# Where the softmax of a differential attention, its filler's vector work and the modulation rows stand in the issue order

## Chip, cores, metric

One core of one Trainium2 chip (trn2). The metric is the device time of one execution in microseconds (us), the median over runs of the same kernel. Engines: PE (TensorE, matmuls), DVE (VectorE), ACT (ScalarE), POOL (GpSimd), SP (which here issues most of the loads). Each engine works through its own queue in order and waits on semaphores for the others.

## What is computed

One layer of a decoder trunk on x of 512 x 1024 (fp32): a modulated RMSNorm, one input projection that feeds two token mixers (sliding-window attention A, differential attention B), a gated merge, and a gated MLP with a short causal convolution. Cut to what matters here:

```python
mod = cs @ w_ada[l] + b_ada[l]                      # 6 x 1024 modulation values
shift1, scale1, gate1, shift2, scale2, gate2 = ...
h = _rmsnorm(x, norm1_g[l]) * (1.0 + scale1) + shift1
proj = h @ w_in[l]
qa, ka, va, qd, kd, vd, ga, gd = jnp.split(proj, points, axis=-1)
...
# _diff_attention, for each block of 128 queries, 4 heads, 2 maps (m) of 64 dimensions
scores = jnp.einsum('bqhmd,bshmd->bhmqs', qblk, k).astype(jnp.float32) * scale
scores = scores - slopes[:, None, None, None] * delta.astype(jnp.float32)
scores = jnp.where(delta >= 0, scores, NEG_INF)
p = jax.nn.softmax(scores, axis=-1)
a = p[:, :, 0] - lam * p[:, :, 1]
return jnp.einsum('bhqs,bshe->bqhe', a.astype(v.dtype), v)
```

The change computes the same.

## The kernel before

**Products.** Every fp32 product is made of three matmuls (`mm3`, L118 to L120): each operand is split into a high part `hi`, an ACT cast to the matmul's type, and a low part `lo = src - hi`, a DVE subtraction (`split`, L114 and L115). PE multiplies weight hi by activation hi (L118), weight hi by activation lo (L119) and weight lo by activation hi (L120); only the third reads the low part of the weight. Weight chunks of 512 KB come by `load_cols` (L464): a raw buffer (tag `raw`, four buffers, shared with the modulation rows), a load on SP, then the split into `whi` and `wlo` (three buffers each).

**The stage.** PE's order in the stage is written by hand (`tc.manual_schedule`); the queues of the other engines are ordered by a scheduler from program order, priorities and dependencies. `tc.high_priority` raises what is traced in it. Small attention matmuls alternate with big ones: `fill(n)` gives out n ticks. A tick runs the next step of the current unit (one k-step of a projection chunk: the query, key and value chunks of the next head `pq`, `pk`, `pw`, or a gate chunk `pga` and a branch chunk `pA`) and keeps two more units' weights loaded ahead. A tick also counts down the callbacks of `after(n, fn)`, and every eighth tick (`ADA_EVERY`) advances the generator `ada_rows` by one step.

**Modulation rows.** The MLP's modulation values are not needed in the attention stage, and `ada_rows` makes them piece by piece: eight half rows of 512 columns (`arow` 00, 01, 10 ... in the text: row, half). A step loads two 128 x 512 slices of `w_ada` (`ra`, L741, on SP), and DVE multiplies each by its value of `cs` and adds it to `arow` (L746, L748). After four steps the half row is split into `arh` and `arl` (L115), and one tick later (`ADA_LAG`) `ada_spread` sums over the partitions by two matmuls on PE (`pr`, L757 for `arh`, L758 for `arl`), ACT copies the row out (L760) and POOL writes it to `mod_rows` (L761). `arow` has one buffer: a new half row begins when the one before has been written.

**Differential attention.** The loop at the end of the listing goes over 16 blocks s = 4h + n (head h, block n of 128 queries). `diff_scores` makes the two maps' scores on PE (L125) and reduces each to its maximum on DVE while adding the mask and the distance penalty (L664; the tile is `sd`, the maximum `dmx`). `diff_softmax` scales the maximum (L676), takes two exponentials on ACT with their sums (L678), and combines the maps on DVE (L681 to L684); L684 leaves the block's probabilities. `diff_transpose` turns them on PE (`td`, L693) and splits them into `aTh` (ACT, L424) and `aTl` (DVE, L425). `diff_values` multiplies by the values (`od`). In a turn of the loop, before: two filler ticks; the scores of the block or blocks ahead; four filler ticks; the transposes of s; the softmax of the block or blocks ahead; in a head's first block also the values of the head before, and two ticks. Ahead of the loop: the scores and softmaxes of blocks 0 and 1, then three ticks.

Of the kernel before, what the change touches and what calls it, by code (L numbers as in the profile page):

```python
# [11 lines left out]
ALU = mybir.AluOpType  # L12
# [15 lines left out]
HP = 100000  # L28
# [8 lines left out]
DIFF_FILL = (3, 2, 4, 2)  # L37
# [15 lines left out]
def kernel(  # L53
# [22 lines left out]
    nc = tc.nc  # L76
# [15 lines left out]
    def fbank(name):  # L92
        return bank("f", 2, [P, S], name)

    def sbank(name, shape=(P, S)):
        return bank("s", 3, list(shape), name)
# [7 lines left out]
    def raw_tile(shape, name):  # L104
        return wp.tile(shape, F32, tag="raw", bufs=4, name=name)

    def split_pair(raw, shape, name):
        hi = wp.tile(shape, F32R, tag="whi", bufs=WB, name=name + "_h")
        lo = wp.tile(shape, F32R, tag="wlo", bufs=WB, name=name + "_l")
        split(hi, lo, raw)  # L110
        return hi, lo
# [10 lines left out]
    def mm3_rows(groups):  # L122
        for a, b, start, stop in ((0, 0, True, False), (0, 1, False, False), (1, 0, False, True)):
            for o, lhs, rhs in groups:
                nc.tensor.matmul(o, lhs[a], rhs[b], start=start, stop=stop)  # L125
# [251 lines left out]
    for gi, g in enumerate(groups):  # L377
        nxt = groups[gi + 1] if gi + 1 < len(groups) else ()
# [83 lines left out]
    def load_cols(src, col, name):  # L462
        r = raw_tile([P, KT, P], name)
        nc.sync.dma_start(r, src[:, col : col + P].rearrange("(a p) n -> p a n", p=P))  # L464
        return split_pair(r, [P, KT, P], name)
# [11 lines left out]
    def prefetch():  # L477
        while units and len(loaded) < 2:
            load, run = units.pop(0)
            loaded.append((load(), run))  # L480

    def fill(n):
        for _ in range(n):
            if not current:
                prefetch()
                if loaded:
                    wts, run = loaded.pop(0)
                    current.append(run(wts))
                    prefetch()
            if current:  # L490
                try:
                    next(current[0])
                except StopIteration:
                    current.clear()
            for e in list(later):
                e[0] -= 1
                if e[0] <= 0:
                    later.remove(e)
                    e[1]()
            tick[0] += 1  # L500
            if tick[0] >= ADA_START and tick[0] % ADA_EVERY == 0:
                next(ada, None)

    def after(n, fn):
        later.append([n, fn])
# [1 line left out]
    def steps(o, wts, rhs, nk, k0=0, cl=slice(0, P)):  # L507
        wh, wl = wts
        for k in range(nk):
            mm3(o, wh[:, k, cl], wl[:, k, cl], rhs[0][k0 + k], rhs[1][k0 + k], k == 0, k == nk - 1)  # L510
            if k < nk - 1:
                yield
# [126 lines left out]
    def diff_scores(*ss):  # L639
        ops = []  # L640
        for s in ss:
            h, n = divmod(s, NT)
            t = heads[h]
            w = (n + 1) * P
            if n == 0:
                firsts[h] = [sbank(f"sd{h}_{m}", (P, 2, 256)) for m in range(2)]
            sps = [firsts[h][m][:, n, :w] if n < 2 else sbank(f"sd{h}_{n}_{m}")[:, :w] for m in range(2)]
            mm3_rows([
                (
                    sps[m],  # L650
                    [t[64 * m : 64 * m + 64, b, n * P : (n + 1) * P] for b in range(2)],
                    [t[64 * m : 64 * m + 64, 2 + b, :w] for b in range(2)],
                )
                for m in range(2)
            ])
            ops.append((s, sps, w))
        for s, sps, w in ops:
            h, n = divmod(s, NT)
            mx = ap.tile([P, 2], F32, tag="dmx", bufs=3, name=f"dmx{h}_{n}")
            pm = []  # L660
            for m in range(2):
                st = ap.tile([P, w], F32, tag="st", bufs=ST, name=f"sd{h}_{n}_{m}")
                with tc.high_priority(offset=HP):
                    nc.vector.tensor_tensor_reduce(  # L664
                        st, sps[m], ddf[:, 512 - w : 512], 1.0, -3e38, ALU.add, ALU.max, mx[:, m : m + 1]
                    )
                pm.append(st)
            scored[s] = mx, pm

    def diff_softmax(s):  # L670
        with tc.high_priority(offset=HP):
            h, n = divmod(s, NT)
            slope = 2.0 ** (-2 * (h + 1))
            mx, pm = scored[s]
            lsum = ap.tile([P, 2], F32, tag="dls", bufs=3, name=f"dls{h}_{n}")
            nc.vector.tensor_scalar_mul(mx, mx, -slope)  # L676
            for m in range(2):
                nc.scalar.activation(  # L678
                    pm[m], pm[m], AF.Exp, bias=mx[:, m : m + 1], scale=slope, accum_out=lsum[:, m : m + 1]
                )  # L680
            nc.vector.reciprocal(lsum, lsum)  # L681
            nc.vector.tensor_mul(lsum[:, 1:2], lsum[:, 1:2], nlam)
            nc.vector.tensor_scalar_mul(pm[1], pm[1], lsum[:, 1:2])
            nc.vector.scalar_tensor_tensor(pm[0], pm[0], lsum[:, 0:1], pm[1], ALU.mult, ALU.add)  # L684
            probs[s] = pm[0]

    def diff_transpose(s):
        h, n = divmod(s, NT)
        if n == 0:
            aTs[h] = [ap.tile([P, 1664], F32R, tag=g, bufs=2, name=f"{g}{h}") for g in ("aTh", "aTl")]  # L690
        tp = tbank(f"td{h}_{n}")
        for k in range(n + 1):
            nc.tensor.transpose(tp[:, k * P : (k + 1) * P], probs[s][:, k * P : (k + 1) * P], ident)  # L693
        hi, lo = (a.rearrange("p (b q) -> p b q", q=P)[:, n : 4 * n + 1 : 3] for a in aTs[h])
        with tc.high_priority(offset=HP):
            evac(hi, lo, tp[:, : (n + 1) * P].rearrange("p (k q) -> p k q", q=P))
# [69 lines left out]
    def add_gate_a(j):  # L766
        def gate(wts):
            o = fbank(f"pga{j}")
            yield from steps(o, wts, hT, KT)
            nc.scalar.activation(ta[:, j], o, AF.Tanh, scale=0.5)  # L770

        def load():
            if j % 2 == 0:
                r = raw_tile([P, 4, 2 * P], f"wba{j}")
                for a in range(2):
                    nc.sync.dma_start(
                        r[64 * a : 64 * a + 64],
                        wba[256 * a : 256 * a + 256, j * P : (j + 2) * P].rearrange("(i p) n -> p i n", p=64),
                    )
                pair_w["a"] = split_pair(r, [P, 4, 2 * P], f"wba{j}")  # L780
            return pair_w["a"]

        def branch(wts):
            o = fbank(f"pA{j}")
            rhs = [[outa[b][:, k] for k in range(4)] for b in range(2)]
            yield from steps(o, wts, rhs, 4, cl=slice(j % 2 * P, j % 2 * P + P))
            nc.vector.scalar_tensor_tensor(ta[:, j], ta[:, j], 1.0, o, ALU.add, ALU.mult)

        units.append((lambda: load_cols(win, COL_GA + j * P, f"wga{j}"), gate))
        units.append((load, branch))  # L790

    pairs, firsts, scored, probs, aTs = {}, {}, {}, {}, {}
    ada = ada_rows()
    add_head(0)
    add_head(1)
    fill(SWA_FILL[0])
    swa_scores(0, 0)
    fill(SWA_FILL[1])
    swa_scores(0, 2)
    swa_softmax(0)  # L800
    fill(SWA_FILL[2])
    for i in range(SWA_PAIRS):
        more = i + 1 < SWA_PAIRS
# [18 lines left out]
    ta = big.tile([P, KT, S], F32, tag="qa", name="ta")  # L822
    for j in range(2):
        add_gate_a(j)
    diff_scores(0, 1)
    diff_softmax(0)
    diff_softmax(1)
    fill(DIFF_FILL[0])
    for s in range(4 * DIFF_HEADS):
        h, n = divmod(s, NT)  # L830
        if n == 0 and 0 < h < 3:
            add_head(h + 1)
        elif s == 12:
            add_gate_a(2)
            add_gate_a(3)
        fill(DIFF_FILL[1])
        nxt = {0: (), 1: (s + 1,), 2: (s + 1,), 3: (s + 1, s + 2)}[n] if s < 15 else ()
        if nxt:
            diff_scores(*nxt)
        fill(DIFF_FILL[2])  # L840
        diff_transpose(s)
        for z in nxt:
            diff_softmax(z)
        if n == 0 and h:
            diff_values(h - 1)
            fill(DIFF_FILL[3])
    for j in range(4, KT):
        add_gate_a(j)
    fill(1)
# [923 lines left out]
```

## Time and profile before

| | us |
|---|---|
| median of 3 runs | 718.32 (717.43 to 718.40) |
| profiled execution | 719.43 |
| its span | 717.4 |
| PE busy | 690.6 |
| DVE busy | 588.9 |
| ACT busy | 383.6 |
| mean granted clock | 0.995 |

The span is what the profiler saw of the program; the profiled execution's time has 2.0 us more around it. The stage that the change touches lies between about 128 and 240 us of the span. In the profile's rows, `td<-ident,sd` means that the operation writes tile `td` and reads `ident` and `sd`; `[1.00 <-DVE qa L428]` is idle time ahead of the row and what ended it. The busy time of a matmul overlaps with its neighbours, since they are pipelined; the distance from one start to the next tells the rate: 0.23 us for a product of 512 columns in this stage.

### The profile page before, as it was taken

The page shows a single profiled execution, that of the slowest core. Times are in us where ns is not written, and L with a number is a line of the kernel's source. Part 1 is how long each engine was busy: PE and PEld are TensorE (multiplying, and loading weights), DVE is VectorE, ACT ScalarE, POOL GpSimd, SP SyncE. Part 2 cuts the span into 40 slices and gives each one's busy share as a digit, 9 for nine tenths or more (in the row PEclk, how much of TensorE's full clock was granted, in tenths as well). Part 3 has the DMA queues.
Part 4 walks back from the last instruction along what each step waited for, and adds up shares of the span by engine and source line. Part 5 has one row for each costly group of instructions (what it writes and reads, how often), then busy time and mean ns, then how long its engine had stood idle before and what let it go on. Part 6 is the DMA issues. An engine that isn't in the chain of part 4 may idle for free. (4 is left out here: it accounts for less than half of the span.)

```text
span 717.4 us, 11279 instructions
## 1 busy us (share of the span) xinstructions
PE 690.6 (96%) x4187; PEld 603.1 (84%) x4187; DVE 588.9 (82%) x1125; ACT 383.6 (53%) x677; POOL 84.0 (12%) x101
## 2 busy tenths in 40 slices
PE   5998899999999999999999999999999999999995
PEld 5776788877887888888879999999999999888884
DVE  5998877887986674875379999888889899979996
ACT  4643656455554233432358665556555666655664
POOL 4000000000100110000012021111111101540300
PEclk9999999999999999999999999999999999999998
DMA  9986122534544565726817689878779738997903
GB/s 310 301 251 205 60 59 61 176 110 126 176 114 151 183 195 182 233 90 211 245 52 156 157 179 210 200 187 219 190 191 230 168 121 237 183 203 194 161 0 118
DMA packets 115863, 121.82 MB, mean 170 GB/s; under 512 B 4415, under 2 KB 93280, under 8 KB 115808
## 3 DMA queue, kind: packets, MB, share of 16 engines
q1 hardware_dynamic: 96894, 95.09, 41.7%
q0 software_dynamic: 18720, 25.73, 21.4%
q8 instruction: 33, 0.54, 0.3%
q10 hardware_dynamic: 194, 0.28, 0.1%
q14 instruction: 22, 0.18, 0.1%
HBM read 118.97 MB, written 2.11 MB: 169 GB/s over the span
## 5 line engine op out<-in xcount | busy, mean ns | idle before, releaser
L1112 PE MATMUL up<-t,m_whi 128*128 128x256 f32 x528 | 96.1, 283 | 0.0
L1112 PEld LDWEIGHTS up<-t,m_whi 128*128 128x128 f32 x528 | 82.3, 192 | 0.0
L1112 PE MATMUL up<-t,m_wlo 128*128 128x256 f32 x264 | 74.7, 283 | 0.1
L1112 PE MATMUL up<-bh,p_wlo 128*128 128x256 f32 x232 | 65.7, 284 | 0.7 <-DVE p_wlo L1055 0.7
L1112 PE MATMUL up<-bh,p_whi 128*128 128x256 f32 x232 | 65.6, 283 | 0.0
L1112 PE MATMUL up<-bl,p_whi 128*128 128x256 f32 x232 | 65.6, 283 | 0.0
L1112 PEld LDWEIGHTS up<-t,m_wlo 128*128 128x128 f32 x264 | 50.6, 192 | 0.3 <-DVE m_wlo L1055 0.3
L1112 PEld LDWEIGHTS up<-bh,p_wlo 128*128 128x128 f32 x232 | 44.4, 192 | 1.1 <-DVE p_wlo L1055 1.1
L1112 PEld LDWEIGHTS up<-bl,p_whi 128*128 128x128 f32 x232 | 44.5, 192 | 0.0
L1112 PEld LDWEIGHTS up<-bh,p_whi 128*128 128x128 f32 x232 | 44.5, 192 | 0.0
L748 DVE SCALAR_TENSOR_TENSOR arow<-ra,cs,arow 128x512 f32<-128x512 f32 x56 | 41.9, 748 | 3.0 <-DMA ra<-in_w_ada_dram 2.3
L1023 POOL DMA_DIRECT2D s<-in_w_up_dram x21 | 27.2, 1385 | 143.2 <-DMA s<-in_w_up_dram 61.0
L1055 DVE TENSOR_TENSOR m_wlo<-s,m_whi 128x1024 fp32r<-128x1024 f32 x31 | 37.8, 1220 | 2.0 <-ACT m_whi L1051 2.0
L1051 ACT CAST m_whi<-s 128x1024 fp32r<-128x1024 f32 x31 | 32.4, 1046 | 9.4 <-DVE s L1045 6.0
L1112 PE MATMUL up<-t,p_whi 128*128 128x256 f32 x176 | 32.2, 283 | 0.0
L174 POOL TENSOR_TENSOR r<-ms,mhalf 128x1 f32<-128x1 f32 (+1 forms) x16 | 13.1, 820 | 143.2 <-DVE ms L172 76.5
L678 ACT ACTIVATE sd<-sd,dmx 128x128 f32<-128x128 f32 (+3 forms) x32 | 17.8, 557 | 22.1 <-DVE dmx L676 15.3
L761 POOL DMA_DIRECT2D mod_rows<-arow x8 | 4.3, 540 | 205.2 <-ACT arow L760 205.1
L1112 PEld LDWEIGHTS up<-t,p_whi 128*128 128x128 f32 x176 | 27.4, 192 | 0.2 <-issue 0.2
L1119 ACT ACTIVATE gT<-a,cv 128x512 f32<-128x512 f32 x22 | 17.7, 813 | 17.7 <-DVE a L1154 17.3
L1051 ACT CAST p_whi<-wa 128x1024 fp32r<-128x1024 f32 x18 | 18.7, 1040 | 12.0 <-PE up L1112 9.0
L1112 PE MATMUL up<-t,p_wlo 128*128 128x256 f32 x88 | 24.9, 283 | 0.0
(485 smaller groups left out, 2119.3 us busy)
## 6 DMA issues: line engine op xcount, KB each, us to landing
ra<-in_w_ada_dram SPq DMA_DIRECT2D x32, 512.0 KB, 4.0
wa<-in_w_up_dram SPq DMA_DIRECT2D x22, 512.0 KB, 4.3
s<-in_w_up_dram SPq DMA_DIRECT2D x21, 512.0 KB, 4.9
s<-in_w_up_dram POOLq DMA_DIRECT2D x21, 512.0 KB, 7.3
adaw<-in_w_ada_dram SPq DMA_DIRECT2D x16, 512.0 KB, 5.3
w<-in_w_in_dram SPq DMA_DIRECT2D x12, 512.0 KB, 3.9
a<-in_w_up_dram SPq DMA_DIRECT2D x11, 512.0 KB, 4.9
b<-in_w_down_dram SPq DMA_DIRECT2D x10, 512.0 KB, 3.8
```

The lines of the kernel that those rows point to most:

```text
L174: nc.gpsimd.tensor_tensor(r0, ms, mhalf[:, :n], ALU.pow)
L678: nc.scalar.activation(pm[m], pm[m], AF.Exp, bias=mx[:, m : m + 1], scale=slope, accum_out=lsum[:, m : m + 1])
L748: nc.vector.scalar_tensor_tensor(ac, r[:, a], cc, ac, ALU.mult, ALU.add)
L761: nc.gpsimd.dma_start(mod_rows[idx : idx + 1, hf * S : (hf + 1) * S], row)
L1023: nc.gpsimd.dma_start(dst, upblock(*blk), accum_op=ALU.add)
L1051: nc.scalar.copy(W[J, name][0], R[J, SRC[name]])
L1055: nc.vector.tensor_sub(lo, R[J, SRC[name]], hi.bitcast(F32))
L1112: nc.tensor.matmul(o[u], w[:, k, cu], b[:, k], start=name in ("p1", "m5", "p2") and k == 0 and x == 0, stop=k == 3 and x == 2, skip_group_ ...
L1119: nc.scalar.activation(grow(j), av[J][:, u], AF.Identity, bias=cv[:, 66 + j : 67 + j], scale=cv[:, 44 + j : 45 + j])
```

## The change

Five edits, all in issue order:

1. `diff_softmax` of the blocks ahead is called right behind their `diff_scores`, no longer behind the filler and the transposes.
2. `ends[s]` keeps the last DVE instruction of a softmax (L684 of before), `ends[s, "exp"]` its last exponential on ACT.
3. What is issued within `tc.issue_after(x)` and goes to the engine of instruction x is put behind x in that engine's queue. The fillers behind the scores (and the first three ticks) are issued within `issue_after(ends[...])` of the first of the new softmaxes.
4. In a head's block 1, the softmax itself is put behind that of block 0, on DVE and on ACT.
5. During the loop (`hold`), a step of `ada_rows` that a tick would run is only counted; `ada_due` runs the counted steps ahead of the four filler ticks, within `issue_after`.

```diff
--- before.py
+++ after.py
@@ -499,7 +499,16 @@
                     e[1]()
             tick[0] += 1
             if tick[0] >= ADA_START and tick[0] % ADA_EVERY == 0:
-                next(ada, None)
+                due[0] += 1
+                if not hold[0]:
+                    ada_due()
+
+    due, hold = [0], [False]
+
+    def ada_due():
+        while due[0]:
+            due[0] -= 1
+            next(ada, None)
 
     def after(n, fn):
         later.append([n, fn])
@@ -668,20 +677,23 @@
             scored[s] = mx, pm
 
     def diff_softmax(s):
-        with tc.high_priority(offset=HP):
+        with tc.high_priority(offset=HP), ExitStack() as order:
             h, n = divmod(s, NT)
+            if n == 1:
+                for key in (s - 1, (s - 1, "exp")):
+                    order.enter_context(tc.issue_after(ends[key]))
             slope = 2.0 ** (-2 * (h + 1))
             mx, pm = scored[s]
             lsum = ap.tile([P, 2], F32, tag="dls", bufs=3, name=f"dls{h}_{n}")
             nc.vector.tensor_scalar_mul(mx, mx, -slope)
             for m in range(2):
-                nc.scalar.activation(
+                ends[s, "exp"] = nc.scalar.activation(
                     pm[m], pm[m], AF.Exp, bias=mx[:, m : m + 1], scale=slope, accum_out=lsum[:, m : m + 1]
-                )
+                ).ins
             nc.vector.reciprocal(lsum, lsum)
             nc.vector.tensor_mul(lsum[:, 1:2], lsum[:, 1:2], nlam)
             nc.vector.tensor_scalar_mul(pm[1], pm[1], lsum[:, 1:2])
-            nc.vector.scalar_tensor_tensor(pm[0], pm[0], lsum[:, 0:1], pm[1], ALU.mult, ALU.add)
+            ends[s] = nc.vector.scalar_tensor_tensor(pm[0], pm[0], lsum[:, 0:1], pm[1], ALU.mult, ALU.add).ins
             probs[s] = pm[0]
 
     def diff_transpose(s):
@@ -789,7 +801,7 @@
         units.append((lambda: load_cols(win, COL_GA + j * P, f"wga{j}"), gate))
         units.append((load, branch))
 
-    pairs, firsts, scored, probs, aTs = {}, {}, {}, {}, {}
+    pairs, firsts, scored, probs, aTs, ends = {}, {}, {}, {}, {}, {}
     ada = ada_rows()
     add_head(0)
     add_head(1)
@@ -822,10 +834,12 @@
     ta = big.tile([P, KT, S], F32, tag="qa", name="ta")
     for j in range(2):
         add_gate_a(j)
+    hold[0] = True
     diff_scores(0, 1)
     diff_softmax(0)
     diff_softmax(1)
-    fill(DIFF_FILL[0])
+    with tc.issue_after(ends[0]):
+        fill(DIFF_FILL[0])
     for s in range(4 * DIFF_HEADS):
         h, n = divmod(s, NT)
         if n == 0 and 0 < h < 3:
@@ -837,13 +851,16 @@
         nxt = {0: (), 1: (s + 1,), 2: (s + 1,), 3: (s + 1, s + 2)}[n] if s < 15 else ()
         if nxt:
             diff_scores(*nxt)
-        fill(DIFF_FILL[2])
+            for z in nxt:
+                diff_softmax(z)
+        with tc.issue_after(ends[nxt[0]]) if nxt else ExitStack():
+            ada_due()
+            fill(DIFF_FILL[2])
         diff_transpose(s)
-        for z in nxt:
-            diff_softmax(z)
         if n == 0 and h:
             diff_values(h - 1)
             fill(DIFF_FILL[3])
+    hold[0] = False
     for j in range(4, KT):
         add_gate_a(j)
     fill(1)
```

## The prediction

> **What bounds the kernel now.** I read the page's busy times first, then its clock row, then the busy times of four stretches, then the waits of TensorE (PE) in the stretch of the change (128 to 240 us), and last the engines' timelines.
>
> ```profile
> PE 690.6 (96%) x4187; PEld 603.1 (84%) x4187; DVE 588.9 (82%) x1125; ACT 383.6 (53%) x677; POOL 84.0 (12%) x101
> PEclk9999999999999999999999999999999999999998
> ```
>
> PE is busy 96% of the span at almost full clock, so any time in which PE stands still is added to the end, unless PE waits later anyway and catches up there.
>
> ```profile
> 60.00:72.00 12.00, 9.66 (x50) 6.76 (x49) 8.82 (x22) 3.34 (x7) 0.00 (x0) 0.86 0.73 229
> 128.00:240.00 112.00, 109.93 (x586) 87.39 (x585) 90.82 (x242) 56.03 (x127) 7.79 (x9) 1.00 0.46 137
> 240.00:330.00 90.00, 90.00 (x400) 74.41 (x400) 63.66 (x79) 31.89 (x42) 3.78 (x8) 1.00 0.57 180
> ```
>
> Columns: stretch, its length, busy us of PE, weight load, DVE, ACT, POOL, then granted clock, DMA share, GB/s. In the differential attention PE idles 2.07 of 112 us; the 90 us behind it have no idle time at all. Nothing behind the stage absorbs a delay.
>
> ```profile
> PE td L693 <- DVE sd L684: 1.6, 3, 1.1
> PE od L119 <- DVE aTl L425: 0.5, 1, 0.5
> ```
>
> These are all of PE's waits there (total, times, longest). Measured from one matmul's start to the next, against its neighbours, they are 1.27 us (155.36 to 156.86), 0.34, 0.49 and 0.88 us: 3.0 us. That is the most the change can win.
>
> **The change.** It adds no arithmetic and no transfer; it adds order. (1) Each softmax is issued right behind its scores, before the filler matmuls. (2) All that the fillers issue on DVE (weight splits at L115, evacuations) is queued behind that softmax's last DVE instruction, L684. (3) Modulation-row steps that fall due are held until that point, so row loads (SP), multiply-adds (L746, L748), the row's split (`arl`, L115) and its two matmuls (`pr`, L757/L758) move. (4) Block 1's softmax comes behind block 0's on DVE and ACT. In the built program's queues PE's order changes at three places only: the `pr` matmuls of rows 01, 10 and 11 come later. SP's order changes in two pairs of loads; but SP and PE wait for what DVE now does later. I walked through the queues, wait by wait, with durations of the profiled execution.
>
> *First stall.* PE's third matmul of the first gate chunk (L120) reads `wga_l`:
>
> ```profile
> 129.66 0.50 PE L118 MATMUL pga<-hThA,wga_h 128*128 128x512 f32 x1
> 130.00 0.39 PE L119 MATMUL pga<-hTlA,wga_h 128*128 128x512 f32 x1
> 130.23 0.39 PE L120 MATMUL pga<-hThA,wga_l 128*128 128x512 f32 x1
> ```
>
> Before, that split was long done, and DVE's softmax came when it suited:
>
> ```profile
> 107.82 1.23 DVE L115 TENSOR_TENSOR wga_l<-wga,wga_h 128x1024 fp32r<-128x1024 f32 x1
> 131.62 0.28 DVE L664 CUSTOM_DVE_ANT_0 sd<-sd,ddf 128x128 f32<-128x128 f32 x1
> 132.72 0.16 DVE L676 TENSOR_SCALAR dmx<-dmx 128x2 f32<-128x2 f32 x1
> 133.84 0.17 DVE L681 RECIPROCAL dls<-dls 128x2 f32<-128x2 f32 x1 [0.22 <-ACT sd L678]
> 134.55 0.35 DVE L684 SCALAR_TENSOR_TENSOR sd<-sd,dls,sd 128x128 f32<-128x128 f32 x1
> 135.49 0.69 DVE L115 TENSOR_TENSOR arl<-arow,arh 128x512 fp32r<-128x512 f32 x1
> ```
>
> Now the split stands behind L684 of block 0. L684 itself is no earlier: the buffer of `wga0` is not freed, so the load of `wga1` waits for a row buffer, as this one does, issued 0.04 us after the DVE instruction that freed it:
>
> ```profile
> 125.31 0.37 SPq L741 DMA_DIRECT2D ra<-in_w_ada_dram  x1
> ```
>
> Loads of 512 KB landed 3.6 to 5.4 us after issue, median 3.9. So `wga1` lands at 129.2 instead of about 113, ACT's cast of it (1.05 us) and of the first attention's output (0.58) end at 130.8, DVE's `outal` at 131.5; the row load queued behind on SP, issued at 127.7, lands at 131.6, and its multiply-add comes next on DVE. Then four score reductions (1.1 us), and from `dmx` at 133.5 the distances of the rows above (132.72 to the end of L684 at 134.90: 2.2 us) give 135.7; the split ends at 136.95. PE is to go on at 136.95 instead of 130.23: **+6.7 us**. If the load lands as early as any, 0.3 less; at 5.4 us, 1.5 more. With every input already there, reductions (from 130.3, PE's last score) 1.1 + 2.2 + 1.2 still leave 4.6, the lower bound.
>
> *Second stall.* `pr` of row 01 moves from 146.34 to behind the scores of head 1's block 0 (149.31 to 150.20) and one step of `pA1`. Its second matmul reads `arl`, now behind L684 of that softmax. ACT's cast of a value weight (1.05 us) stands before the exponentials and waits for `pA1`; DVE's split of it (1.22) stands before the reciprocal; then reciprocal to L684 1.0, `dmx` 0.1, `arl` 0.69. From the end of the scores that is 4.1 us beyond what PE has to do: **+4.1**, between 3.2 (without the cast and split before the softmax: reductions 1.1, `dmx` 0.2, two exponentials of 0.40, 1.0, 0.69, less 0.6 of PE's own matmuls) and 5 (the reductions wait as well). In return the wait at 155.36, for this very softmax, is gone: **-1.3**, and the one at 176.05: **-0.3**.
>
> *Third stall.* `pr` of row 10 moves back by three steps, its `arl` waits for ACT's cast `arh` and the split behind a softmax: **+1.7**, bounds 0 and 3. One `td` of head 2: **+0.2**.
>
> *Fourth stall.* `pr` of row 11 moves from 204.87 to just behind the scores of head 3's block 2 (213.3 plus lateness, 224.2). Between those scores and `arl` lie two reductions of 384 columns (1.0), `dmx` 0.2, two exponentials (0.62 each), reciprocal to L684 1.5 and `arl` 0.69: 4.6 us, one matmul of PE's less. In front stand the split of `wga4` and an evacuation; `wga4` is loaded only when the last multiply-add of row 11 frees a buffer (218.65 + 3.9 + cast 1.05 + split 1.22 + 0.68 = 225.5, that is 1.3 after the scores): **+5.9**, bounds 4.4 and 7.
>
> *The stage's end.* The wait of 0.49 shrinks: **-0.4**. The last `od` waits for `aTl` behind another split and a row step: **+1.3**, bounds 0 and 2.
>
> Sum of waits: 6.7 + 4.1 - 1.6 + 1.7 + 0.2 + 5.9 - 0.4 + 1.3 = **17.9 us**, bounds (the lower and upper ends added up) about 10 and 24.
>
> *The clock.* Before, PE once waited 0.62, 1.00 and 0.27 us within 3.7 us (63.95 to 67.66), and this followed:
>
> ```profile
> 66.29 0.32 PE L125 MATMUL sw<-ka,qa 64*128 64x128 f32 x1 [1.00 <-DVE qa L428]
> 68.31 0.63 PE L120 MATMUL pq<-hThA,w_l 128*128 128x512 f32 x1
> ```
>
> The granted clock was 0.5 from 68.13 to 71.54 us (the 0.86 of the first stretch above); matmuls started 0.42 us apart instead of 0.23: 3.41 us at half clock, a loss of 1.7. No row shows what an unbroken wait of 4 to 7 us does. The first, second and fourth stall are longer than that: from nothing to 3 x 1.7 = 5.1; I take 1.0 each, **+3.0**, nearer to the one case seen than to nothing.
>
> [...]
>
> **Total.** The profiled execution is 719.43 us (span 717.4, 2.0 outside), 1.1 above the median. 719.43 + 17.9 + 3.0 = 740.3; as a median, **739 us**.
>
> **Rivals.**
> *A, the forecast* (731 to 746).
> *B, only part of it is paid.* For it: DVE is busy 81% of the stage and ACT half of it, and each time PE grows late they and the loads get time to catch up, so that the next split is nearer to ready. Then the first stall at its lower bound 4.6, the second at 3.2, nothing for the third, half of the fourth, less the 2.0 won, no clock loss: 4.6 + 3.2 + 2.9 - 2.0 = 8.7, **727**. Against: the fourth is the softmax's own length.
> *C, faster.* PE's 3.0 us of waits in the stage are for softmax (L684) or for what follows it (`aTl`); softmax ahead of DVE's other work ends them all: **715.3**. It decides if the splits queued behind softmax are still done when PE reads them; the queue has the first of them 6.7 us late, which speaks against it.
> *D, worse.* Each stall delays loads that reuse buffers, the next weights come late too, or the clock stays halved past one 3.41 us stretch: waits at their upper bound 24 plus 5.1: **747** or more.
> *E, it does not do what it says.* Softmax and splits start when their inputs arrive, as before, and the new order decides nothing: **718**, within 0.2%. Against: in the queue the splits do stand behind softmax, and 90 us without idle time catch nothing up.
>
> **Chances.** A 0.73, B 0.13, D 0.08, C 0.04, E 0.02. The range reaches from just under B to A's upper end: 726 to 746. About 0.2% can be told from no change here: faster (C) 0.04, same (E) 0.02, slower (A, B, D) 0.94.
>
> **What would show it.** In the changed profile PE should wait at L120 of `pga` for DVE `wga_l` about 6.7 us near 130; at L758 of `pr` for `arl` about 4, 1.7 and 6 us near 158, 188 and 224; waits of `td` for L684 should be nearly gone; the clock should drop behind the long waits; the stage should take 21 us longer, the one behind it no longer than before. I am wrong if `wga_l` is ready near 130, or if the waits are there and a later stage is shorter.

## The result, and the profile after

The changed kernel takes 744.58 us (median of 4 runs, 743.84 to 747.09); the kernel before, run beside it, 718.12 us. The ratio is 1.037, 95% interval 1.035 to 1.040: 26.5 us slower. The profiled execution of the changed kernel took 747.09 us (span 745.0), 27.7 us more than that of the kernel before. One execution of a variant below (e9) took 968.63 us at a mean granted clock of 0.656; its ratio leaves it out (the median of e9 without it is 719.47).

The page's busy row and clock row:

```profile
PE 701.4 (94%) x4187; PEld 611.4 (82%) x4187; DVE 589.2 (79%) x1125; ACT 384.3 (52%) x677; POOL 83.9 (11%) x101
PEclk8999999789998999999999999999999999999998
```

The counted instructions of each engine are as many as before, and DVE works as long; the clock row has dents in the stage (slices of 18.6 us; the stage is slices 7 to 15, the dents 8, 9 and 13). PE's waits between 128 and 262 us (total, times, longest):

```profile
PE pr L770 <- DVE arl L115: 10.6, 3, 6.5
PE pga L120 <- DVE wga_l L115: 6.5, 1, 6.5
PE od L119 <- DVE aTl L425: 1.4, 1, 1.4
PE td L705 <- DVE sd L696: 0.8, 1, 0.8
PE pr L769 <- ACT arh L114: 0.6, 1, 0.6
PE od L118 <- ACT aTh L424: 0.2, 1, 0.2
```

The waits for softmax (`td`) have halved, and nearly 18 us of waits for splits of weights and modulation rows stand in their place. (Lines move by 12: L757, L758 and L684 of before are L769, L770 and L696.) Busy time by stretch, with the granted clock behind the POOL column:

```profile
72.00:128.00 56.00, 53.85 (x351) 44.61 (x350) 42.44 (x146) 35.21 (x105) 0.70 (x1) 1.00 0.17 52
128.00:144.00 16.00, 9.53 (x42) 7.32 (x41) 8.69 (x24) 3.51 (x10) 0.00 (x0) 0.68 0.57 173
164.00:172.00 8.00, 7.73 (x25) 6.24 (x26) 4.66 (x10) 1.98 (x6) 0.51 (x1) 0.63 0.38 121
228.00:242.00 14.00, 7.55 (x29) 5.49 (x28) 6.84 (x15) 4.01 (x9) 0.55 (x1) 0.76 0.15 41
262.00:350.00 88.00, 88.00 (x395) 72.91 (x394) 60.84 (x79) 32.33 (x43) 5.68 (x10) 1.00 0.59 183
```

At the stage's start the two profiled executions are level (the matmul at 109.71 us before starts at 109.66 now), but by a coincidence: the changed one ran at half clock from 12.95 to 19.77 us and was some 1.5 us late until 68 us, where the one before had its own 3.41 us at half clock. In the variants below the first scores (`sd`), here at 128.72 us, start anywhere between 125.4 and 128.9 us. So profiled executions are compared from the start of the first scores to the end of the span: 588.6 us before, 616.3 now, which is the 27.7 us. Behind the stage PE has no idle time for 88 us, as before, and all of the loss lies in the stage. The first stall, PE's timeline:

```profile
129.94 0.40 PE L119 MATMUL pga<-hTlA,wga_h 128*128 128x512 f32 x1
136.81 0.80 PE L120 MATMUL pga<-hThA,wga_l 128*128 128x512 f32 x1 [6.47 <-DVE wga_l L115]
137.41 0.63 PE L118 MATMUL pga<-hThA,wga_h 128*128 128x512 f32 x1
137.84 0.63 PE L119 MATMUL pga<-hTlA,wga_h 128*128 128x512 f32 x1
```

and what SP, ACT and DVE did meanwhile (rows in between left out):

```profile
125.25 0.39 SPq L464 DMA_DIRECT2D wga<-in_w_in_dram  x1
129.18 1.05 ACT L114 CAST wga_h<-wga 128x1024 fp32r<-128x1024 f32 x1 [2.53 <-DMA wga<-in_w_in_dram]
130.74 0.69 DVE L425 TENSOR_TENSOR outal<-oa,outah 128x512 fp32r<-128x512 f32 x1 [3.01 <-ACT outah L424]
131.60 0.75 DVE L760 SCALAR_TENSOR_TENSOR arow<-ra,cs,arow 128x512 f32<-128x512 f32 x1 [0.17 <-DMA ra<-in_w_ada_dram]
133.38 0.16 DVE L688 TENSOR_SCALAR dmx<-dmx 128x2 f32<-128x2 f32 x1
135.21 0.35 DVE L696 SCALAR_TENSOR_TENSOR sd<-sd,dls,sd 128x128 f32<-128x128 f32 x1
135.54 1.22 DVE L115 TENSOR_TENSOR wga_l<-wga,wga_h 128x1024 fp32r<-128x1024 f32 x1
```

This is the chain that the prediction walked through: the load of the next gate weight issued at 125.25 because a buffer is not free earlier, ACT's casts and DVE idle for 3.01 us behind it, the row step, the reductions, softmax, and only then the split, which DVE had done at 107.82 before. After it PE's 512-column matmuls start 0.43 us apart instead of 0.23: the granted clock is 0.50 until 142.65.

### The profile page after: what moved, and what is told of

The parts are those of the page before. It is cut to its first block, busy times and chain, and to the rows that moved or that the text cites. A ratio compares the mean times of both kernels' runs of the same rounds, so it can differ in the third digit from the quotient of the medians.

```text
span 745.0 us, 11263 instructions
## 1 busy us (share of the span) xinstructions
PE 701.4 (94%) x4187; PEld 611.4 (82%) x4187; DVE 589.2 (79%) x1125; ACT 384.3 (52%) x677; POOL 83.9 (11%) x101
## 5 line engine op out<-in xcount | busy, mean ns | idle before, releaser
L120 PE MATMUL pga<-hThA,wga_l 128*128 128x512 f32 x48 | 20.9, 434 | 6.5 <-DVE wga_l L115 6.5
L1136 ACT ACTIVATE gT<-a,cv 128x512 f32<-128x512 f32 x22 | 17.7, 813 | 17.6 <-DVE a L1171 17.3
L1068 ACT CAST p_whi<-wa 128x1024 fp32r<-128x1024 f32 x18 | 18.7, 1041 | 12.1 <-PE up L1129 9.0
```

Source lines behind the costliest of these rows:

```text
L120: nc.tensor.matmul(o, ll, rh, start=False, stop=stop)
L1068: nc.scalar.copy(W[J, name][0], R[J, SRC[name]])
L1136: nc.scalar.activation(grow(j), av[J][:, u], AF.Identity, bias=cv[:, 66 + j : 67 + j], scale=cv[:, 44 + j : 45 + j])
```

## The experiments

Eleven variants of the two kernels, each timed against the kernel before on the same chip:

| kernel | median us | ratio to before, 95% | profiled, first scores to end, us (before: 588.6) |
|---|---|---|---|
| changed | 744.58 | 1.037 (1.035 to 1.040) | 616.3 |
| e1 first ticks free | 733.71 | 1.023 (1.020 to 1.025) | 605.0 |
| e2 rows at their ticks | 736.41 | 1.027 (1.025 to 1.029) | 607.7 |
| e7 both | 729.11 | 1.015 (1.012 to 1.019) | 599.2 |
| e9 first ticks and rows outside the order | 719.63 | 1.002 (1.001 to 1.004) | 589.3 |
| e6 no order on fillers | 720.46 | 1.004 (1.002 to 1.006) | 591.0 |
| e8 e1, rows read later | 727.73 | 1.014 (1.012 to 1.017) | 598.8 |
| e3 only the softmax moved | 718.55 | 1.002 (1.001 to 1.003) | 588.5 |
| e5 useless matmuls in the waits | 735.17 | 1.025 (1.024 to 1.027) | 606.8 |
| c1 fewer of them | 740.47 | 1.031 (1.028 to 1.033) | 605.7 |
| f1 rows behind the filler | 720.34 | 1.004 (1.003 to 1.005) | 590.0 |
| f3 f1 with ADA_LAG 2 | 723.05 | 1.006 (1.004 to 1.009) | 591.3 |

The medians of the kernel before, taken beside the variants, lie between 717.2 and 718.2 us, so differences between medians of different rows are good to about 1 us.

**e1: is the first stall the order on the first ticks?**

```diff
-    with tc.issue_after(ends[0]):
-        fill(DIFF_FILL[0])
+    fill(DIFF_FILL[0])
```

> The changed kernel, but the first three filler ticks are no longer issued within issue_after, so the split of the first gate chunk's weight is not queued behind block 0's softmax. Theory (each late split or row costs its own wait plus a stretch at half clock behind it): TensorE's wait of 6.5 us at L120 of pga is gone and the half clock behind it (5.8 us, a loss of 2.8) with it; the other waits (4.1, 1.3 and 6.6 us) stay as they are; 744.6 - 6.6 - 2.8 = 735 us. Rival (VectorE as a whole is behind, and one wait that goes only lengthens the next): the wait at pr of row 01 grows by most of what is saved, 742 to 745 us.

733.71 us, 10.9 less than the changed kernel (9.4 were expected), and the other waits stayed:

```profile
PE pr L770 <- DVE arl L115: 10.3, 3, 6.2
PE od L119 <- DVE aTl L425: 1.4, 1, 1.4
```

The wait for `wga_l` is gone and none has grown: a stall that goes does not pass its time on to the next. The rival falls. More was gained than expected: from the first scores to the end 11.3 us, 1.9 above the 9.4. If the half clock behind the `od` wait (1.6 us in the changed kernel) is gone too, though that wait is as long as there (1.4 us), it makes up most of this; that is an estimate from these times.

**e2 and e7: is it the holding of the rows?**

```diff
-    hold[0] = True
+    hold[0] = False
```

> The changed kernel, but the modulation-row steps run at their ticks as in the kernel before; the order behind softmax stays for all that the four fillers issue. Theory: the first stall stays (6.5 us and 2.8 of half clock); the waits of pr for arl (4.1 + 0.5, 6.6) and for arh (0.8) and the half clock behind the two long ones (2.4 + 2.1) go: 744.6 - 12.0 - 4.5 = 728 us, up to 731 if a row's split that still falls into a filler behind softmax waits about 2 us. Rival (the rows are not the cause, the order behind softmax of weight splits and evacuations is): above 738 us.

736.41 us, between the two. PE's waits:

```profile
PE pr L770 <- DVE arl L115: 8.4, 2, 5.0
PE pga L120 <- DVE wga_l L115: 6.2, 1, 6.2
```

The stall of row 11 is gone, but rows 01 and 10 wait 3.4 and 5.0 us: at their own ticks these two rows' splits fall into a filler that is ordered behind a softmax, and PE reads them one tick later. My upper figure of 731 had allowed 2 us for such a split. Together with e1's edit:

> The changed kernel with the first ticks free and the rows at their ticks (e1 and e2 together). e2 still showed pr waits of 5.0 and 3.4 us, since two rows' splits fall into fillers behind softmax. Theory (the stalls are separate and add): e2 less the first stall and its half clock, 736.4 - 6.2 - 2.8 = 727.4 us. Rival (one stall gives the others time to catch up): 731 us or more, with pr waits longer than in e2.

729.11 us, between the theory's 727.4 and the rival's 731; the `pr` waits are 7.8 us instead of 8.4, so they have not grown, as the rival would have it. The order without the holding thus still costs 11.6 us; e6 below, the holding without the order, costs 2.9. Most of it is the order.

**e9: rows outside the order, weights still in it.**

```diff
-        with tc.issue_after(ends[nxt[0]]) if nxt else ExitStack():
-            ada_due()
+        ada_due()
+        with tc.issue_after(ends[nxt[0]]) if nxt else ExitStack():
             fill(DIFF_FILL[2])
```

(and e1's edit)

> The changed kernel with two things outside issue_after: the first three filler ticks, and the counted modulation-row steps (ada_due), which still run behind the softmax in program order. TensorE's order is that of the changed kernel, and weight splits and evacuations of the four fillers stay queued behind softmax. Theory (beyond the first stall, the rows' splits queued behind a softmax are the whole loss): of e1's time the waits of pr (4.1, 1.3 and 6.3 us) and the half clock behind two of them (2.4 + 2.1) go: 733.7 - 16.2 = 717.5 us, no wait of pr left over 0.3 us. Rival (weight splits behind softmax cost as much by themselves, hidden so far by the rows' waits): 722 to 728 us with new waits of TensorE for L115 of w, wga or wba.

719.63 us; 14.1 us less than e1. PE's waits in the stage:

```profile
PE td L705 <- DVE sd L696: 3.4, 3, 2.2
PE od L119 <- DVE aTl L425: 0.2, 1, 0.2
```

No `pr` wait is left, and no weight split is waited for, though the later fillers' splits are still queued behind softmax. Two things taken out of the order, the first weight and the rows, account for some 24 of the 26.5 us (e9 is 2.1 us above the kernel before beside it). What is left shows as a new wait of 2.2 us of `td` in head 3: DVE did four row multiply-adds of 0.75 us and a weight split between that block's reductions and L696; in the kernel before it was one multiply-add and the split of a row, and this wait was 0.3 us.

**e6: no order on fillers at all.** (e1's edit, and `ExitStack()` in place of `issue_after` in the loop.)

> The changed kernel without any issue_after around fillers; softmax early, rows held and block 1 behind block 0 stay. Theory (the order behind softmax is the cause, holding rows by itself is not): 717 to 719 us. Rival (rows held and then done in one burst crowd VectorE): above 722 us, with waits of td for L696 or of pr for arl.

720.46 us, between theory and rival. PE waited 4.1 us for softmax (three times, longest 3.1). Holding the rows is not harmless by itself: in the longest wait, for the same block as in e9 (0.3 us in the kernel before), four row multiply-adds and a weight split stood between the reductions and L696.

**e8: the same DVE order, read later by PE.** (e1's edit, `ADA_LAG = 6`.)

> e1 with ADA_LAG 6 instead of 1: VectorE's order stays as in the change (rows' splits behind softmax), but TensorE reads each split five ticks later. Theory (a split behind softmax costs only because TensorE's fixed order asks for it right behind the scores): the pr waits of rows 01, 10 and 11 shrink to 2 us and less in all, the half clock with them: 717.5 to 722 us. Rival (a late split also holds up what is behind it on VectorE and the row's buffers, so that the delay shows elsewhere): 726 to 734 us.

727.73 us, in the rival's range: 6.0 us less than e1, not 12 to 16. The `pr` waits fell from 10.9 to 4.4 us, but `pss` now waits 1.9 us for DVE (`dmx`): a late split holds up others too. Of the 14.1 us that e9 saves against e1, reading later saves 6.0; the theory fails.

**e3: the softmax alone.** The kernel before, with

```diff
             diff_scores(*nxt)
+        for z in nxt:
+            diff_softmax(z)
         fill(DIFF_FILL[2])
         diff_transpose(s)
-        for z in nxt:
-            diff_softmax(z)
```

> The kernel before, with only the softmax moved right behind its scores: no issue_after, no holding of rows. Theory (moving softmax is harmless or good; the loss is all in the order put on the fillers and the rows): the waits of td for L684 (1.27, 0.34, 0.49 us) shrink and nothing takes their place: 715.5 to 718.2 us. Rival (softmax ahead of evacuations and splits itself makes those late): above 719.5 us, with new waits of TensorE on L115 or L425.

718.55 us against 717.22 beside it: 0.1 to 0.3% slower, in any case not faster. PE's waits in the stage:

```profile
PE td L693 <- DVE sd L684: 2.1, 3, 1.1
PE od L119 <- DVE aTl L425: 0.6, 1, 0.6
```

They are much as before (1.6 and 0.5). Softmax was already traced at high priority (`HP`; the row steps have half of it), and its place in the program changes little. The theory's waits did not shrink. Where the 1.3 us of the median lie was not found: from the first scores to the end the profiled execution takes as long as that of before.

**e5 and c1: is the half clock a cost of its own?** Useless matmuls fill the waits; the real product overwrites them.

```diff
+            for _ in range(28 if j == 0 else 0):
+                nc.tensor.matmul(o, wts[0][:, 0, :P], hT[0][0], start=True, stop=True)
             yield from steps(o, wts, hT, KT)
...
+        for _ in range({(0, 1): 18, (1, 0): 2, (1, 1): 28}.get((idx, hf), 0)):
+            nc.tensor.matmul(pr, onesr, ah, start=True, stop=True)
         nc.tensor.matmul(pr, onesr, ah, start=True, stop=False)
```

> The changed kernel with useless matmuls put where TensorE waits: 28 of 512 columns ahead of the first gate chunk, 18 ahead of pr of row 01, 2 ahead of row 10, 28 ahead of row 11 (0.227 us each, 17.3 us in all), each overwritten by the real product, so the output is unchanged. Theory (the half clock follows from TensorE's standing still): the waits are filled, not shortened, the clock stays at 1.0 behind all three, and 2.8 + 2.4 + 2.1 = 7.3 us are saved: 737 us, faster by adding work. Rival 1 (the half clock has another cause, or costs nothing because the late splits would hold TensorE anyway): 744 to 746 us. Rival 2 (the waits are not waits, and the extra matmuls add to the end): 755 to 762 us.

735.17 us: 76 matmuls of no use (17.3 us of PE) make the kernel 9.4 us faster in the median, 8.5 with each taken against the kernel before beside it, and 9.4 in the profiled executions from the first scores to the end. The granted clock of the stage:

```profile
128.00:250.00 122.00, 118.74 (x608) 93.78 (x607) 89.42 (x235) 53.43 (x123) 5.99 (x6) 1.00 0.40 120
```

It is 1.00 over these 122 us, where the changed kernel had the clock at half for 10.24, 6.83 and 6.83 us behind the three waits. The splits that PE waits for come hardly earlier by this: counted from the first matmul of `pga`, useless ones included, `wga_l` is ready after 7.0 us (7.2 in the changed kernel); counted from the first of `pr`, those of rows 01 and 11 are ready after 4.3 and 6.3 us (4.3 and 6.8). What has changed is the clock. The 18.2 us that e5 takes longer than the kernel before from the first scores on are about the sum of the waits alone. Then with part of the useless matmuls:

> e5 with fewer useless matmuls: 14, 12, 2 and 20 instead of 28, 18, 2 and 28, so that TensorE stands still for about 3.3, 1.4, 0.8 to 1.4 and 2 us. The sum of waits and useless work is that of e5 (735.2 us), so what is above it is the clock. [...] Rival 2 (any of these waits drops it, as the sum of three short waits did in the kernel before): three drops, 741 us and more.

740.47 us in the median, but five executions from 733.53 (mean clock 0.996) to 742.77 (0.985), the other three at 0.987. The profiled one was the fastest, and shows no drop around its longest wait:

```profile
128.85:132.26 3.41, 1.74 (x8) 1.12 (x6) 3.01 (x15) 0.88 (x4) 0.00 (x0) 1.00 0.02 4
132.26:135.67 3.41, 1.89 (x8) 1.57 (x9) 3.41 (x6) 1.09 (x4) 0.00 (x0) 1.00 0.69 185
```

Here the clock stayed at 1.00 through both stretches of the wait of 3.3 us (1.8 us of it in the first, 1.5 in the second) and in the 3.42 us behind them; the other four executions have no profile, so which wait halved their clock is not shown. By the mean clocks the slowest was at half clock for some 16 us more than the fastest, which is worth up to 8 of the 9.2 us between them. The median lies 5.3 us above the 735.2 of e5, and half a microsecond below rival 2's 741.

**f1 and f3: a version that beats both?** e1's edit, and in the loop

```diff
+        hold[0] = bool(nxt)
         with tc.issue_after(ends[nxt[0]]) if nxt else ExitStack():
-            ada_due()
             fill(DIFF_FILL[2])
+        hold[0] = False
+        ada_due()
```

without `hold[0] = True` ahead of it.

> A try to beat both: softmax early and four fillers ordered behind it as in the change; first ticks free; rows run at their ticks, but those that fall due in an ordered filler are held until it is over and run outside the order. Theory: e7 had td waits for softmax of 0.2 us in all (before: 1.6 by the same view) and e9 had no pr waits; both together leave some 0.8 us of waits in the stage, against 3.0 before: 717.5 - 2.2 = 715.3 us, 714.5 to 716.5. Rival (rows that are free of the order push themselves ahead of a later softmax, as in e9): td waits of 2 us and more come back, 717 to 720 us.

720.34 us, just above the rival's range: no `pr` wait, but 2.3 us of `td` and 1.6 us of `od`.

> f1 with ADA_LAG 2, so that a row's matmuls come one tick later. Theory: where f1 shows no pr wait, this is the same within 0.5 us; where f1 shows one (row 11, for arh), it is gone here. Rival (the row's buffer is freed later and the next row's steps crowd into the next softmax): 1 us and more slower than f1.

723.05 us, 2.7 slower than f1, as its rival had it. No variant beats the kernel before; DVE is busy 81% of that stage, and in each order tried some operand of PE came late.

## Why the prediction was right, and where it was off

Forecast 739, measured 744.6, in the range. Step by step, from the starts of the same matmuls in both profiled executions (us):

| step | forecast | measured |
|---|---|---|
| first stall, `wga_l` | +6.7 | +6.6 |
| second, `arl` of row 01 | +4.1 | +4.1 |
| waits gone (`td`) | -1.6 | -1.6 |
| third, row 10 | +1.7 | +1.3 (0.8 for `arh`, 0.5 for `arl`) |
| `td` of head 2 | +0.2 | +1.0 |
| fourth, `arl` of row 11 | +5.9 | +6.6 |
| stage's end, `td` and `od` | +0.9 | +0.7 |
| sum of waits | +17.9 | +18.7 |
| half clock | +3.0 | +9.4 (2.8, 2.7, 2.3, 1.6) |

The two make 28.1 of the 28.3 us by which the stage grew; 0.6 of that comes back behind the stage, where a wait of 0.7 us for `xn` (L1197 before) is gone, and 27.7 remain between the profiled executions. In the medians it is 26.5: the profiled execution had the lowest mean clock (0.974) of the four, the others 0.978 to 0.981.

- **The mechanism was right**, and its places: walking the built queues, wait by wait, gave the first stall's end to 0.2 us (136.95 forecast, 136.81). e1 and e9 show that the two orders, on the first weight and on the rows' splits, are what costs. That the `pr` waits for `arl` are 4.0, 0.2 and 6.5 us, where 4, 1.7 and 6 were named, and that the third stall is for the most part one for `arh`, are small misses.
- **The fourth stall** was 0.7 longer: the load of `wga4`, issued at 224.57, was cast only at 229.25, and DVE idled 3.48 us for it.
- **The mis-sized step was the clock**: "I take 1.0 each, **+3.0**". It cost 9.4 us in the profiled execution, above the upper bound of 5.1, and e5 got this back. Of the 6.8 us by which the profiled execution lies above the sum for it (740.3), 6.4 are this term; the range of 726 to 746 still held, by 1.4 us, and as far as the clock goes that was luck. The one drop seen before had cost 1.7 us: PE was at work again at 67.66 us, the clock was at half from 68.13 to 71.54, and PE kept at work through it. In the three long stalls the drop began while PE still stood (at 132.41, 163.13 and 234.81 us; PE went on at 136.81, 164.27 and 236.87), and full clock came back at 142.65, 169.96 and 241.64, which is 4.8 to 5.8 us behind PE's restart. And a fourth drop came that was not counted, from 255.29 to 258.71 us, behind the two `od` waits:

```profile
252.34 0.49 PE L118 MATMUL od<-aTh,qkv 128*128 128x512 f32 x1 [0.25 <-ACT aTh L424]
254.19 0.50 PE L119 MATMUL od<-aTl,qkv 128*128 128x512 f32 x1 [1.36 <-DVE aTl L425]
251.88:255.29 3.41, 1.81 (x8) 1.20 (x8) 3.41 (x5) 0.41 (x1) 0.00 (x0) 1.00 0.34 71
255.29:258.71 3.42, 3.42 (x13) 2.94 (x13) 3.38 (x5) 1.18 (x2) 0.00 (x0) 0.50 0.98 346
```

In the 3.41 us from 251.88 PE stood still for 2.04 us, counted from the starts of its matmuls, and half clock followed.

- **Rival B** (DVE catches up, 727) fell: e1 left the other stalls as they were. **C** fell by e3: the softmax's earlier place won nothing, though the waits that it was said to end did shrink in the changed kernel, by 1.6 us, where the fillers were held back. **D** had the clock's behaviour right, "halved past one 3.41 us stretch" (three of the four drops lasted longer: 10.24, 6.83 and 6.83 us), and its price was nearer the truth than mine; its waits at their upper bound and its late weights beyond the stage did not come. **E** fell with the waits themselves.

## What to carry to other kernels

An order put on "the rest" of an in-order engine also orders the operands that another engine, with a fixed order of its own, reads next; before adding it, list who reads each held result, and when. Price a wait of TensorE with the half clock that may follow it (here waits of 6.5, 4.0, 6.5 and 1.4 us had 2.8, 2.7, 2.3 and 1.6 us of it on top), and to see what of a loss is the clock, fill the wait with useless matmuls. Moving work earlier on an engine that is 81% busy can move something else later: it did in every order tried here.

## What the runs showed of the hardware

In the profiled execution of the kernel before, the granted clock was at half from 68.13 to 71.54 us and for the last 4.1 us of the span; in that of the changed kernel from 12.95 to 19.77, 132.41 to 142.65, 163.13 to 169.96, 234.81 to 241.64 and 255.29 to 258.71 us, and for the last 5.0. Busy time and clock of the changed kernel in five stretches of 3.41 us, around the first stall:

```profile
129.01:132.42 3.41, 1.33 (x14) 0.76 (x12) 1.51 (x3) 1.53 (x2) 0.00 (x0) 1.00 0.43 145
132.42:135.83 3.41, 0.00 (x0) 0.00 (x0) 3.01 (x16) 1.04 (x5) 0.00 (x0) 0.50 0.14 20
135.83:139.25 3.42, 2.44 (x6) 1.96 (x7) 3.38 (x6) 0.93 (x4) 0.00 (x0) 0.50 0.66 214
139.25:142.65 3.40, 3.40 (x10) 2.63 (x9) 0.78 (x2) 0.00 (x0) 0.00 (x0) 0.50 0.99 309
142.65:146.06 3.41, 3.41 (x19) 2.79 (x18) 0.69 (x1) 1.45 (x3) 0.00 (x0) 1.00 0.24 72
```

In the first stretch PE was idle for 2.25 us (from one matmul's start to the next, less the usual distance at the clock of the moment, which is 0.23 or 0.43 us for 512 columns), and at its end the clock was halved. In the third, idle for 1.15 us, and in the fourth, with matmuls 0.43 us apart throughout, it was 0.50; in the fifth it was 1.00. Counted so, without pieces of up to 0.15 us, PE was idle for 2.99, 3.41 and 2.04 us in the 3.41 us ahead of the other three drops of this stage (at 163.13, 234.81 and 255.29 us). In c1 the two stretches with 1.83 and 1.52 us of idle time, and the one behind them, have 1.00; in e9 so have the 3.41 us from 223.97 with 1.88 us of it and the 3.42 us behind them.

The length of a wait alone does not tell what follows it: behind the `od` wait of some 1.4 us in the changed kernel the clock was at half for 3.41 us, and behind the wait of 3.2 us in c1 it was not. The five executions of c1 (733.5 to 742.8 us) have mean clocks from 0.996 down to 0.985; what spread them is not shown, since one alone was profiled.
